# A recorder that counts TensorE's instructions in blocks of 256, and HGRN2 levels as single steps, in a hybrid decoder step

## The chip, the cores and the metric

The kernel runs on one core of one Trainium2 chip. The metric is the device time of one launch in microseconds (us). The kernel before takes 838.85 us, the median of 3 runs (838.39 to 838.94).

## What is computed

One inference step of a decoder layer for 544 token columns: a prompt of 512 tokens and 8 samples of 4 new tokens each, all in float32. The reference, cut to what matters here:

```python
h = rmsnorm(x, norm_mix); z = h @ w_in
aq, ak, av, hq, hf, hi, hg = jnp.split(z, IN_SPLITS, axis=-1)
att = dilated_attention(aq, k_all, v_all, q_idx)              # 8 heads, prompt and cached window
f = lb + (1.0 - lb) * jax.nn.sigmoid(hf)
o, s_new = hgrn2_recurrence(silu(hq) * HG_DK ** -0.5, 1.0 - f, hi, jnp.log(f), hg_s0)   # 4 heads
o = head_rmsnorm(o, hg_out_norm) * silu(hg)
x = x + concatenate([att, o]) @ w_out
x = x + cross_attention(rmsnorm(x, norm_cross), mem_k, mem_v) @ w_co
u = rmsnorm(x, norm_ffn)
x = x + (silu(causal_conv3(u @ w_gate)) * (u @ w_up)) @ w_down
y = rmsnorm(x, norm_final)
```

## The kernel before, in words

Activations lie with their features on the 128 partitions and the 544 tokens along the free axis. A dense product takes one 128-wide column strip of a weight at a time. Weight and activation are each split into a high and a low part (type fp32r), and three products, high by high, high by low and low by high, are summed in a PSUM bank. The tokens are cut into two parts of 256 and 288 (CUTS), so a *half* of a projection (w_in has 8 contraction tiles) is 24 matmuls. These dense products are the **main** steps of TensorE, and their order is fixed by the program. Everything else on TensorE is a **side** product in plain fp32: attention scores and values (psS, psT, psO), the decode attention over the cached window, whose tiles are streamed in (psd, psdo), cross-attention (ps_cp, ps_cpt, ps_cpo, ps_cs), and the HGRN2 heads.

An HGRN2 head (`hgrn`, one for each h of 0 to 3) works in levels w = 1, 2, 4 ... 64. `level_ops` makes a tile kq on VectorE and GpSimd, and `level_products` multiplies small blocks of it with each other on TensorE: 16 products of 32 columns for the levels up to 16 (one more for the samples at 1 and 2), 8 at level 32, 4 at level 64. They land in the banks psB (the diagonal, levels 1 and 2), psA (4, 8, 16) and psL (32, 64). Then come transposes and state products (pst, psin, psU, psu, pso), a norm (psr_hg), and the result om goes into the contraction of w_out (ps_wo).

The program doesn't issue instructions as it is written. `Tape` records every call as part of a `Step`; consecutive calls on TensorE of one kind (main or side) join into one step until `tape.cut()`. `Tape.order` then plays through all five engines with its own cost figures, and `Tape.run` issues the instructions in the order of the best of four such rounds. In that play TensorE takes the next main step in order, and side steps in between where they are ready:

```python
can = [s for s in waiting["PE"] if s.ready <= now + 1e-9 and fits(s)]
main = [s for s in can if s.main]
side = [s for s in can if not s.main]
if side and (burst or not main or sum(s.length for s in side) >= self.BURST
             or now - first > self.PATIENCE
             or min(s.begin for s in side) < clock[0] + now - clock[1]):
```

Each engine then has one list that it works off in order, and buffers (the tag "a" has 59) are handed out in the planned order, so a change in one list can move the others. Because every instruction is issued through `take`, nearly all rows of the profile carry its line, L621 (L597 for the DMAs).

The feed-forward stage computes gate and up projections: the first tiles plainly (ps_g, ps_u), the rest in pairs with seven block products in place of eight (ps_ag, ps_au, ps_cg, ps_cu, ps_dg, ps_du). Their weight operands S1 and S3 are sums of two blocks: one load on the SP queue, and a second, adding one on GpSimd's queue (POOL). VectorE forms S2 and S4 from them, and ScalarE (ACT) and VectorE split all of them into high and low parts (S1u4h, S2u4h, S2u4l). The products with w_down (ps_d, last ps_dz) stand between these; their activations are the tiles h0, h1 ..., split as h3h, h3l. `keep` copies a partial product out of its bank (keptg) before the bank's next product, such as S1 by T, is added.

Of the kernel before, what the change touches and what calls it, by code (L numbers as in the profile page):

```python
# [235 lines left out]
class Step:  # L236


    def __init__(self, engine, number, main):
        self.engine, self.number, self.main = engine, number, main  # L240
        self.calls, self.length, self.lag, self.bytes, self.port = [], 0.0, 0.2, 0, False
        self.deps, self.users, self.tiles = set(), [], set()
        self.gate, self.lead, self.after = None, None, set()

# [5 lines left out]
class Tape:  # L250
# [6 lines left out]

    ROUNDS = 4
    BURST, PATIENCE, SLACK, LEAD, MARGIN = 1.0, 4.0, 12.0, 15.0, 4.0
    AHEAD = {"SP": 8, "ACT": 5, "DVE": 5, "POOL": 5, "PE": 8}  # L260

    def __init__(self, nc):
# [27 lines left out]
        dims = tuple(tuple(d) for d in ap.ap)  # L290
        return name, p0, p0 + dims[0][1], _bits(dims[1:]) << f0

    def put(self, engine, call, outs, ins, length, lag=None, size=0, port=False):
        main = self.in_main and engine == "PE"
        cur = self.cur
        if not (cur is not None and cur.engine == engine and cur.main == main and (engine == "PE" or self.joined)):
            cur = self.cur = Step(engine, len(self.steps), main)
# [15 lines left out]
        cur.length += length  # L313
        cur.bytes += size
        cur.port |= port
        if lag is not None:
            cur.lag = lag
        for ap, write in [(a, False) for a in ins] + [(a, True) for a in outs]:
# [109 lines left out]
    def order(self):  # L428
# [22 lines left out]


        port = [0.0, 0.0]

        def needs(s):
            want = {}
# [24 lines left out]
            return True  # L481

        def start(s):
            nonlocal todo, bus
            waiting[s.engine].remove(s)
            for k, v in needs(s).items():
                room[k] -= v
            for n in s.tiles:
                if n in last and n not in held:
                    ends[n] = last[n]  # L490
            held.update(n for n in s.tiles if n in self.kinds)
            s.start = now
            if s.bytes:
                free[s.engine] = now + 0.4
                bus = max(bus, now) + s.bytes / 300e3
                s.end = bus + 2.0
            else:
                held_up = max(0.0, port[s.engine == "DVE"] - now) if s.port else 0.0
                if s.port:
                    port[s.engine == "POOL"] = now + held_up + s.length  # L500
                free[s.engine] = s.end = now + held_up + s.length
            if s.main:
                clock[:] = s.est, now
            for n in s.tiles:
                if n in self.kinds:
                    left[n] -= 1
                    if not left[n]:
                        ends.pop(n, None)
                        frees.append((s.end + s.lag, self.kinds[n]))
            todo -= 1  # L510
            done.append(s)
            seen = set()
            for u in s.users:
                if u in seen:
                    continue
                seen.add(u)
                if s not in u.deps:
                    at = s.start
                elif u.engine == s.engine and not s.bytes:
                    at = s.start + s.length - 0.05  # L520
                else:
                    at = s.end + s.lag
                u.ready = max(u.ready, at)
                u.waits -= 1
                if not u.waits:
                    waiting[u.engine].append(u)

        while todo:
# [12 lines left out]
            if free["PE"] <= now + 1e-9:  # L541
                can = [s for s in waiting["PE"] if s.ready <= now + 1e-9 and fits(s)]
                main = [s for s in can if s.main]
                side = [s for s in can if not s.main]
                if side and first is None:
                    first = now
                if side and (burst or not main or sum(s.length for s in side) >= self.BURST
# [15 lines left out]
                    moved = True  # L563
            if not moved:
                later = [f[0] for f in frees] + [free[e] for e in free if free[e] > now + 1e-9]
                later += [s.ready for e in waiting for s in waiting[e] if s.ready > now + 1e-9]
                if not later and self.idle < 40:

                    self.idle, clock[0] = self.idle + 1, clock[0] + 1.0
                    continue  # L570
                self.idle = 0
                assert later, "no step can begin"
                now = min(t for t in later if t > now + 1e-9)
# [3 lines left out]
class _Engine:  # L577
# [5 lines left out]
    def __getattr__(self, method):  # L583
# [3 lines left out]
        def take(*args, **kw):  # L587
# [3 lines left out]
            outs = [a for a in [kw.get("out", args[0] if args else None), kw.get("accum_out")] if hasattr(a, "ap")]  # L591
            ins = [a for a in aps if not any(a is o for o in outs)]
            n = max([int(np.prod(a.shape[1:])) for a in aps] + [1])
            lag, size, port = 0.25, 0, False
            if method == "dma_start":
                size = 4 * int(np.prod(outs[0].shape))
                return tape.put(engine, lambda: call(*args, **kw), outs, ins, 0.1, 0.3, size)  # L597
            if engine == "PE":
                n, m, k = int(np.prod(args[2].shape[1:])), outs[0].shape[0], args[1].shape[0]
                if method == "transpose":  # L600
                    n, length = 128, 0.11
                elif args[1].dtype == F32R:
                    length = 0.00046 * n + 0.001
                else:
                    length = 2 * max(0.0135, 0.00086 * n * (m / 128 if m < 128 else 1.0) * (0.5 if k <= 64 else 1.0))
                lag = 0.35
# [10 lines left out]
            else:  # L617
                port = True
                length = {"tensor_tensor": 0.2 + 0.0026 * n, "memset": 0.15 + 0.0007 * n,
                          "tensor_scalar": 0.2 + 0.0036 * n}.get(method, 0.45 + 0.0009 * n)  # L620
            return tape.put(engine, lambda: call(*args, **kw), outs, ins, length, lag, size, port)  # L621
        return take


# [1 line left out]
def tile_decoder_step(ctx: ExitStack, tc: tile.TileContext, xT, memT, kwT, vw, s0, conv_in, mkT, mv, vecs, cst,  # L626
# [619 lines left out]
    def hgrn(h, f, q, gt, v):  # L1246
# [42 lines left out]
            return kq  # L1289

        def level_products(w, kq):
            if w <= 2:
                diag_blocks(kq, kq, bank["b"], w)
                diag_sample(kq, kq, w)
# [223 lines left out]
    x = []  # L1518
# [733 lines left out]
```

## Time and profile before

| | |
|---|---|
| median of 3 runs | 838.85 us (838.39 to 838.94) |
| the profiled execution's own time | 839.05 us |
| its span in the profile | 837.3 us |
| TensorE matmuls (PE), weight loads (PEld) | 820.8 us (98%), 768.2 us (92%) |
| VectorE (DVE), ScalarE (ACT), GpSimd (POOL) | 584.8 us (70%), 398.9 us (48%), 139.0 us (17%) |

The profile is one execution, taken by the hardware profiler. Busy time is the union of an engine's instructions; matmuls are pipelined, so their rows overlap. A wait is idle time of an engine before an instruction, with what ended it: another engine's instruction, a DMA, or "issue", when the profile shows nothing that was waited for. SPq is the queue of SyncE, which issues most DMAs. Times in timelines are us from the start of the span.

### The profile page before, as it was taken

The page shows a single profiled execution, that of the slowest core. Times are in us where ns is not written, and L with a number is a line of the kernel's source. Part 1 is how long each engine was busy: PE and PEld are TensorE (multiplying, and loading weights), DVE is VectorE, ACT ScalarE, POOL GpSimd, SP SyncE. Part 2 cuts the span into 40 slices and gives each one's busy share as a digit, 9 for nine tenths or more (in the row PEclk, how much of TensorE's full clock was granted, in tenths as well). Part 3 has the DMA queues.
Part 4 walks back from the last instruction along what each step waited for, and adds up shares of the span by engine and source line. Part 5 has one row for each costly group of instructions (what it writes and reads, how often), then busy time and mean ns, then how long its engine had stood idle before and what let it go on. Part 6 is the DMA issues. An engine that isn't in the chain of part 4 may idle for free.

```text
span 837.3 us, 18858 instructions
## 1 busy us (share of the span) xinstructions
PE 820.8 (98%) x7599; PEld 768.2 (92%) x7599; DVE 584.8 (70%) x1246; ACT 398.9 (48%) x793; POOL 139.0 (17%) x239
## 2 busy tenths in 40 slices
PE   9999999999989999999999999999999999999996
PEld 9988888878788978999889998999999999999995
DVE  6775634956869996564475998977677667767754
ACT  7422323533627635453444557554455545545533
POOL 1120000110110110232133122012011210210013
PEclk9999999999999999999999999999999999999998
DMA  9647777874942544343640247556546644654503
GB/s 334 208 137 205 229 251 246 277 238 149 301 150 69 183 128 123 111 148 115 196 153 27 76 102 216 127 137 182 135 114 163 169 122 116 175 150 90 162 1 107
DMA packets 90760, 132.32 MB, mean 158 GB/s; under 512 B 6065, under 2 KB 60081, under 8 KB 90545
## 3 DMA queue, kind: packets, MB, share of 16 engines
q1 hardware_dynamic: 84480, 120.69, 45.1%
q0 software_dynamic: 5184, 9.44, 7.0%
q8 instruction: 59, 0.97, 0.4%
q10 hardware_dynamic: 1008, 0.99, 0.4%
q14 instruction: 29, 0.23, 0.1%
HBM read 123.03 MB, written 8.07 MB: 157 GB/s over the span
## 4 chain that ended last, share of the span: by engine, by line
PE 94%; DMA 3%; ACT 1%; issue 1%; DVE 0%; ACTq 0%; DVEq 0%
PE ps_d L621 13%; PE ps_au L621 6%; PE ps_ag L621 6%; PE ps_wo L621 6%; PE ps_cu L621 3%; PE ps_cg L621 3%; PE ps_k L621 3%; PE ps_q L621 3%; PE ps_hv L621 3%; PE ps_co L621 3%; PE ps_cq L621 3%; PE ps_g L621 3%; PE ps_dz L621 3%; PE ps_v L621 3%; PE ps_u L621 3%; PE ps_hf L621 2%
## 5 line engine op out<-in xcount | busy, mean ns | idle before, releaser
L621 ACT CAST wh<-wr 128x1024 fp32r<-128x1024 f32 (+1 forms) x68 | 60.9, 908 | 127.6 <-issue 15.9
L621 DVE TENSOR_TENSOR wl<-wr,wh 128x1024 fp32r<-128x1024 f32 (+1 forms) x68 | 73.1, 1085 | 13.8 <-ACT wh L621 13.3
L621 DVE TENSOR_TENSOR xr<-xr,ps_d 128x256 f32<-128x256 f32 x80 | 34.4, 433 | 36.7 <-PE ps_d L621 36.4
L621 POOL TENSOR_TENSOR hG<-hG,hf 128x256 f32<-128x256 f32 (+1 forms) x28 | 24.5, 877 | 204.9 <-DVE hf L621 132.7
L621 DVE SCALAR_TENSOR_TENSOR cv<-ug,vec,cv 128x560 f32<-128x560 f32 x44 | 35.1, 797 | 8.1 <-ACT cv L621 7.8
L621 POOL COPY last<-ug 128x2 f32<-128x2 f32 (+1 forms) x44 | 13.6, 340 | 160.7 <-DVE ug L621 133.5
L621 ACT ACTIVATE cv<-cv 128x560 f32<-128x560 f32 x22 | 14.8, 673 | 19.5 <-DVE cv L621 19.4
L621 ACT ACTIVATE cv<-ug,vec 128x560 f32<-128x560 f32 x22 | 18.8, 856 | 10.3 <-DVE ug L621 9.5
L597 POOL DMA_DIRECT2D S1u<-in_w_up x9 | 7.8, 862 | 87.6 <-DMA S1u<-in_w_up 31.0
L621 POOL TENSOR_TENSOR acc_cx<-acc_cx,sq_cx 128x256 f32<-128x256 f32 (+1 forms) x14 | 11.6, 834 | 61.8 <-ACT sq_cx L621 61.7
L621 ACT ACTIVATE P<-P,mx 128x128 f32<-128x128 f32 (+3 forms) x32 | 17.6, 552 | 5.9 <-DVE mx L621 5.9
L621 PE MATMUL ps_co<-coh,wh 128*128 128x256 f32 (+1 forms) x64 | 19.0, 298 | 0.0
L621 PE MATMUL ps_co<-col,wh 128*128 128x256 f32 (+1 forms) x64 | 18.4, 288 | 0.0
L621 PE MATMUL ps_co<-coh,wl 128*128 128x256 f32 (+1 forms) x64 | 18.4, 288 | 0.0
L621 POOL COPY ug<-conv_state 128x16 f32<-128x16 f32 x22 | 16.5, 751 | 6.1 <-PE ps_u L621 4.2
L621 DVE TENSOR_TENSOR xr<-xr,ps_wo 128x256 f32<-128x256 f32 (+1 forms) x16 | 6.8, 435 | 14.7 <-PE ps_wo L621 14.7
L621 PE MATMUL psd<-st,qbd_win 128*32 128x224 f32 x256 | 16.4, 360 | 0.0
L621 PE MATMUL psdo<-st,dpt 128*32 128x256 f32 x224 | 15.4, 385 | 0.7 <-DMA st<-in_vw 0.7
L621 DVE TENSOR_TENSOR xr<-xr,ps_dz 128x288 f32<-128x288 f32 (+1 forms) x16 | 7.0, 436 | 12.4 <-PE ps_dz L621 12.4
L621 POOL TENSOR_TENSOR acc_ux<-acc_ux,sq_ux 128x256 f32<-128x256 f32 (+1 forms) x14 | 11.9, 848 | 20.8 <-ACT sq_ux L621 20.8
L621 ACT ACT_TABLE_LOAD x11 | 14.1, 1283 | 2.3 <-issue 2.1
L621 DVE CUSTOM_DVE_ANT_0 P<-psS,bias 128x128 f32<-128x128 f32 (+3 forms) x32 | 14.2, 484 | 1.4 <-PE psS L621 1.3
(2650 smaller groups left out, 3561.5 us busy)
## 6 DMA issues: line engine op xcount, KB each, us to landing
st<-in_kwT SPq DMA_DIRECT2D x32, 448.0 KB, 5.0
st<-in_vw SPq DMA_DIRECT2D x28, 512.0 KB, 5.8
wr<-in_w_in SPq DMA_DIRECT2D x25, 512.0 KB, 5.7
wd<-in_w_down SPq DMA_DIRECT2D x32, 256.0 KB, 2.9
wrg<-in_w_gate SPq DMA_DIRECT2D x9, 512.0 KB, 5.5
wru<-in_w_up SPq DMA_DIRECT2D x9, 512.0 KB, 4.8
st<-in_mkT SPq DMA_DIRECT2D x8, 512.0 KB, 5.8
wr<-in_w_out SPq DMA_DIRECT2D x8, 512.0 KB, 3.7
```

The costliest lines, as they stand in the source:

```text
L597: return tape.put(engine, lambda: call(*args, **kw), outs, ins, 0.1, 0.3, size)
L621: return tape.put(engine, lambda: call(*args, **kw), outs, ins, length, lag, size, port)
```

## The change

Each step on TensorE now carries its number of instruction words: 4 for an fp32 product, 2 for an fp32r product or a transpose. `order` adds them up, times 1.0086, and treats the sum as cut into blocks: the first ends after 195 words, each further one after 256. When a step carries the sum over a block's end, the time of that is kept (`block_at`). `fetch` gives the earliest time at which a side step may begin: if it would cross into the next block, or come within 48 words behind such a crossing, not before the last crossing plus 6.6 us. Side steps that are earlier are left out of the choice; main steps are not held. In `level_products` a `tape.cut()` makes each level a step of its own.

```diff
--- before.py
+++ after.py
@@ -238,7 +238,7 @@
 
     def __init__(self, engine, number, main):
         self.engine, self.number, self.main = engine, number, main
-        self.calls, self.length, self.lag, self.bytes, self.port = [], 0.0, 0.2, 0, False
+        self.calls, self.length, self.lag, self.bytes, self.port, self.words = [], 0.0, 0.2, 0, False, 0
         self.deps, self.users, self.tiles = set(), [], set()
         self.gate, self.lead, self.after = None, None, set()
 
@@ -257,6 +257,9 @@
 
     ROUNDS = 4
     BURST, PATIENCE, SLACK, LEAD, MARGIN = 1.0, 4.0, 12.0, 15.0, 4.0
+
+
+    BLOCK, FIRST, WAITS, FETCH = 256, 195, 1.0086, 6.6
     AHEAD = {"SP": 8, "ACT": 5, "DVE": 5, "POOL": 5, "PE": 8}
 
     def __init__(self, nc):
@@ -290,7 +293,7 @@
         dims = tuple(tuple(d) for d in ap.ap)
         return name, p0, p0 + dims[0][1], _bits(dims[1:]) << f0
 
-    def put(self, engine, call, outs, ins, length, lag=None, size=0, port=False):
+    def put(self, engine, call, outs, ins, length, lag=None, size=0, port=False, words=0):
         main = self.in_main and engine == "PE"
         cur = self.cur
         if not (cur is not None and cur.engine == engine and cur.main == main and (engine == "PE" or self.joined)):
@@ -313,6 +316,7 @@
         cur.length += length
         cur.bytes += size
         cur.port |= port
+        cur.words += words
         if lag is not None:
             cur.lag = lag
         for ap, write in [(a, False) for a in ins] + [(a, True) for a in outs]:
@@ -451,6 +455,16 @@
 
 
         port = [0.0, 0.0]
+        words, block_at = 0.0, -100.0
+
+        def fetch(s):
+
+            n, x = s.words * self.WAITS, (self.FIRST - words) % self.BLOCK
+            if not n or x >= n + 48:
+                return 0.0, None
+            if x < n:
+                return block_at + self.FETCH - s.length * x / n, x / n
+            return block_at + self.FETCH - s.length - (x - n) / 16, None
 
         def needs(s):
             want = {}
@@ -481,7 +495,7 @@
             return True
 
         def start(s):
-            nonlocal todo, bus
+            nonlocal todo, bus, words, block_at
             waiting[s.engine].remove(s)
             for k, v in needs(s).items():
                 room[k] -= v
@@ -490,6 +504,10 @@
                     ends[n] = last[n]
             held.update(n for n in s.tiles if n in self.kinds)
             s.start = now
+            if s.words:
+                at = fetch(s)[1]
+                block_at = block_at if at is None else now + s.length * at
+                words += s.words * self.WAITS
             if s.bytes:
                 free[s.engine] = now + 0.4
                 bus = max(bus, now) + s.bytes / 300e3
@@ -541,7 +559,7 @@
             if free["PE"] <= now + 1e-9:
                 can = [s for s in waiting["PE"] if s.ready <= now + 1e-9 and fits(s)]
                 main = [s for s in can if s.main]
-                side = [s for s in can if not s.main]
+                side = [s for s in can if not s.main and fetch(s)[0] <= now + 1e-9]
                 if side and first is None:
                     first = now
                 if side and (burst or not main or sum(s.length for s in side) >= self.BURST
@@ -563,7 +581,7 @@
                     moved = True
             if not moved:
                 later = [f[0] for f in frees] + [free[e] for e in free if free[e] > now + 1e-9]
-                later += [s.ready for e in waiting for s in waiting[e] if s.ready > now + 1e-9]
+                later += [t for e in waiting for s in waiting[e] for t in (s.ready, fetch(s)[0]) if t > now + 1e-9]
                 if not later and self.idle < 40:
 
                     self.idle, clock[0] = self.idle + 1, clock[0] + 1.0
@@ -591,16 +609,17 @@
             outs = [a for a in [kw.get("out", args[0] if args else None), kw.get("accum_out")] if hasattr(a, "ap")]
             ins = [a for a in aps if not any(a is o for o in outs)]
             n = max([int(np.prod(a.shape[1:])) for a in aps] + [1])
-            lag, size, port = 0.25, 0, False
+            lag, size, port, words = 0.25, 0, False, 0
             if method == "dma_start":
                 size = 4 * int(np.prod(outs[0].shape))
                 return tape.put(engine, lambda: call(*args, **kw), outs, ins, 0.1, 0.3, size)
             if engine == "PE":
                 n, m, k = int(np.prod(args[2].shape[1:])), outs[0].shape[0], args[1].shape[0]
+                words = 4
                 if method == "transpose":
-                    n, length = 128, 0.11
+                    n, length, words = 128, 0.11, 2
                 elif args[1].dtype == F32R:
-                    length = 0.00046 * n + 0.001
+                    length, words = 0.00046 * n + 0.001, 2
                 else:
                     length = 2 * max(0.0135, 0.00086 * n * (m / 128 if m < 128 else 1.0) * (0.5 if k <= 64 else 1.0))
                 lag = 0.35
@@ -618,7 +637,7 @@
                 port = True
                 length = {"tensor_tensor": 0.2 + 0.0026 * n, "memset": 0.15 + 0.0007 * n,
                           "tensor_scalar": 0.2 + 0.0036 * n}.get(method, 0.45 + 0.0009 * n)
-            return tape.put(engine, lambda: call(*args, **kw), outs, ins, length, lag, size, port)
+            return tape.put(engine, lambda: call(*args, **kw), outs, ins, length, lag, size, port, words)
         return take
 
 
@@ -1289,6 +1308,7 @@
             return kq
 
         def level_products(w, kq):
+            tape.cut()
             if w <= 2:
                 diag_blocks(kq, kq, bank["b"], w)
                 diag_sample(kq, kq, w)
```

The change moves instructions on every engine. Three places follow. A row is line, operation, tile written and tiles read, shape, and how often; the changed program's `take` has the line L640 (L615 for DMAs).

TensorE, HGRN2 head 0 (psB, psA), the decode stream (psd) and the projections ps_q. Before:

```order
L621 MATMUL ps_q_256_218<-xm7h,wl_216 128x288
L621 MATMUL psB_174<-hq_111,hk_171 32x32 x17
L621 MATMUL psB_174<-kq_1_172 32x32 x17
L621 MATMUL psB_174<-kq_2_173 32x32 x17
L621 MATMUL psA_177<-kq_4_175 32x32 x16
L621 MATMUL psA_177<-kq_8_176 32x32 x16
L621 MATMUL ps_q_0_223<-xm0h,wh_221 128x256
```

and with the change, the 24 products of the half ps_q_256 and the 24 of ps_q_0 left out where the dots are:

```order
L640 MATMUL psB_174<-hq_111,hk_171 32x32 x17
L640 MATMUL pst_hv_190<-cs,hv_163 128x128 x4
L640 MATMUL psB_174<-kq_1_172 32x32 x17
L640 MATMUL psd_238<-st_122,qbd_win 32x224 x4
L640 MATMUL psd_238<-st_123,qbd_win 32x224 x4
L640 MATMUL psB_174<-kq_2_173 32x32 x17
L640 MATMUL ps_q_256_218<-xm0h,wh_215 128x288
...
L640 MATMUL ps_q_0_223<-xm7h,wl_222 128x256
L640 MATMUL psA_177<-kq_4_175 32x32 x16
L640 MATMUL psA_177<-kq_8_176 32x32 x16
```

Five levels in a row became three and two, with two halves of a projection between them; the three of psB begin a half earlier and have a transpose and stream products in between.

TensorE, HGRN2 head 1 (psA_381), with the stream (psdo) and projections of v and of the next head (ps_v, ps_hf). Before:

```order
L621 MATMUL ps_v_256_419<-xm7h,wl_416 128x288
L621 MATMUL psdo_429<-st_495,dpt_427 32x256 x4
L621 MATMUL psA_381<-kq_4_379 32x32 x16
L621 MATMUL psA_381<-kq_8_380 32x32 x16
L621 MATMUL psdo_429<-st_501,dpt_427 32x256 x4
L621 MATMUL pst_v_430<-cs,v_413 128x128 x4
```

and with the change, 45 products of ps_hf left out where the dots are:

```order
L640 MATMUL ps_v_256_419<-xm7h,wl_416 128x288
L640 MATMUL psB_378<-hq_343,hk_375 32x32 x17
L640 MATMUL psB_378<-kq_1_376 32x32 x17
L640 MATMUL psB_378<-kq_2_377 32x32 x17
L640 MATMUL psA_381<-kq_4_379 32x32 x16
L640 MATMUL psdo_429<-st_492,dpt_427 32x256 x4
L640 MATMUL pst_v_430<-cs,v_413 128x128 x4
L640 MATMUL psS_436<-cs,v_413 32x128
L640 MATMUL ps_hf_0_481<-xm0h,wh_479 128x256
...
L640 MATMUL ps_hf_256_484<-xm7h,wl_480 128x288
L640 MATMUL psA_381<-kq_8_380 32x32 x16
L640 MATMUL psA_381<-kq_16_385 32x32 x16
```

Levels 4 and 8 stand apart now, with both halves of ps_hf between them; psB, which stood ahead of the half ps_v_256, stands behind it.

ACT, at the start of the paired part of the feed-forward stage. Before:

```order
L621 CAST wd_0h<-wd_0_1236 128x512
L621 COPY keptg_1205<-ps_ag_1177 128x272
L621 CAST S4g4h<-S4g_1228 128x512
L621 CAST A22g4h<-A22g_1251 128x512
L621 ACTIVATE cv_1162<-cv_1162 128x560
L621 CAST wd_1h<-wd_1_1261 128x512
L621 COPY keptg_1205<-ps_ag_1177 128x272
L621 CAST S1u4h<-S1u_1241 128x512
L621 CAST h3h<-up_1166 128x544
```

and with the change:

```order
L640 CAST S1u4h<-S1u_1241 128x512
L640 COPY keptg_1205<-ps_ag_1177 128x272
L640 CAST S4g4h<-S4g_1228 128x512
L640 CAST whg_1270<-wrg_1269 128x1024
L640 ACTIVATE cv_1162<-cv_1162 128x560
L640 CAST wd_0h<-wd_0_1236 128x512
L640 COPY keptg_1205<-ps_ag_1177 128x272
L640 CAST A22g4h<-A22g_1251 128x512
L640 CAST h3h<-up_1166 128x544
```

S1u4h moved ahead of both copies keptg. On the SP queue, the load that it needs, with the semaphores (named by engine or DMA queue) that each waits for; before:

```order
L597 DMA wru_1223<-in_w_up 128x1024 [waits DMAHW4_49,DMAHW1_49,DVE_49]
L597 DMA S1u_1241<-in_w_up 128x512 [waits PE_49]
L597 DMA wd_0_1236<-in_w_down 128x512 [waits PE_49]
L597 DMA S3u_1247<-in_w_up 128x512 [waits PE_49]
L597 DMA A22g_1251<-in_w_gate 128x512 [waits DMAHW5_49,DVE_49,Pool_49]
```

and with the change:

```order
L615 DMA wru_1223<-in_w_up 128x1024 [waits DMAHW4_49,DVE_49]
L615 DMA S1u_1241<-in_w_up 128x512 [waits DMAHW2_49,DVE_49]
L615 DMA wrg_1269<-in_w_gate 128x1024 [waits DMAHW5_49,Activation_49]
L615 DMA wd_0_1236<-in_w_down 128x512 [waits PE_49]
L615 DMA S3u_1247<-in_w_up 128x512 [waits PE_49]
```

S1u's load no longer waits for TensorE but for VectorE, and the load of wrg moved up behind it.

## Rows read from the trace of the kernel before

**Rows 1.** The page, busy us (share of the span) and instructions of each engine.

```profile
PE 820.8 (98%) x7599; PEld 768.2 (92%) x7599; DVE 584.8 (70%) x1246; ACT 398.9 (48%) x793; POOL 139.0 (17%) x239
```

**Rows 2.** Waits of PE: waiting line, what ended it, us in total, times, longest.

```profile
PE psA L621 <- issue: 5.2, 3, 2.2
...
PE ps_au L621 <- ACT S2u4h L621: 0.8, 1, 0.8
PE psdo L621 <- DMA st<-in_vw: 0.7, 1, 0.7
PE ps_hf L621 <- issue: 0.5, 1, 0.5
PE ps_d L621 <- DVE h3l L621: 0.4, 1, 0.4
PE ps_d L621 <- ACT h3h L621: 0.3, 1, 0.3
PE ps_au L621 <- DVE S2u4l L621: 0.2, 1, 0.2
```

**Rows 3.** Timeline of PE at four gaps: start, us, instruction, [idle before, releaser].

```profile
49.14 0.44 PE L621 MATMUL psA<-kq 128*32 128x32 f32 x26 [1.92 <-issue]
...
171.36 0.29 PE L621 MATMUL psA<-kq 128*32 128x32 f32 x11 [1.07 <-issue]
...
177.04 0.38 PE L621 MATMUL ps_hf<-xm0h,wh 128*128 128x256 f32 x1 [0.49 <-issue]
...
235.83 0.38 PE L621 MATMUL psA<-kq 128*32 128x32 f32 x10 [2.21 <-issue]
```

**Rows 4.** The page, DMA queue of the instructions: packets, MB, share of 16 engines.

```profile
q8 instruction: 59, 0.97, 0.4%
```

**Rows 5.** Stretches between gaps: us, PE, PEld, DVE, ACT, POOL busy (instructions), PEclk, DMA.

```profile
47.30:170.20 122.90, 120.37 (x1399) 102.25 (x1399) 74.28 (x206) 42.05 (x84) 11.20 (x20) 1.00 0.71 226
170.20:176.70 6.50, 5.28 (x137) 4.43 (x127) 4.73 (x9) 1.66 (x7) 2.60 (x4) 1.00 1.05 330
176.70:233.70 57.00, 56.58 (x636) 45.82 (x636) 37.58 (x101) 26.21 (x52) 3.73 (x5) 1.00 0.68 220
```

**Rows 6.** The same view, of the stretches just ahead of three gaps.

```profile
46.00:47.30 1.30, 1.22 (x131) 1.10 (x117) 0.79 (x2) 0.76 (x1) 0.41 (x2) 1.00 0.81 275
165.10:170.20 5.10, 5.10 (x124) 4.33 (x111) 3.65 (x12) 1.00 (x1) 1.90 (x3) 1.00 1.09 351
231.40:233.70 2.30, 2.22 (x129) 1.53 (x115) 2.14 (x5) 1.60 (x4) 0.00 (x0) 1.00 1.13 358
```

**Rows 7.** The chain that ended last, 75 to 86 us: start, us, what.

```profile
75.66 3.39 PE ps_k L621 x24
...
79.56 3.04 PE ps_k L621 x24
```

**Rows 8.** Timeline of PE at 45.5 us, from main to side products.

```profile
45.50 0.29 PE L621 MATMUL ps_q<-xm7h,wl 128*128 128x288 f32 x1
45.72 0.27 PE L621 MATMUL psB<-hq,hk 128*32 128x32 f32 x8
```

**Rows 9.** Waits of SPq, timelines of SP, ACT and PE, and the chain, 495 to 514 us.

```profile
SPq L597 <- PE ps_u L621: 14.9, 2, 14.5
...
501.94 0.33 SPq L597 DMA_DIRECT2D S1u<-in_w_up  x1
...
505.14 8.41 DMA S1u<-in_w_up
...
495.17 0.65 ACT L621 CAST h2h<-up 128x544 fp32r<-128x544 f32 x1 [0.41 <-DVE up L621]
...
507.95 0.38 ACT L621 COPY keptg<-ps_ag 128x272 f32<-128x272 f32 x1
...
513.62 0.62 ACT L621 CAST S1u4h<-S1u 128x512 fp32r<-128x512 f32 x1 [2.64 <-DMA S1u<-in_w_up]
...
508.78 0.28 PE L621 MATMUL ps_ag<-Th,S1g4h 128*128 128x272 f32 x1
```

## The prediction

> **What bounds the kernel now.** First the page's busy times: TensorE's matmuls cover 820.8 of 837.3 us, no other engine more than 70% [rows 1]. The kernel ends when TensorE has worked off its list, so only two things can shorten it: less TensorE work, or less TensorE idling. Second, who TensorE waits for [rows 2]. The rows shown that name another engine or a DMA sum to 2.4 us; two others, 5.2 and 0.5 us, name "issue": nothing that the profile shows was missing. Third, TensorE's timeline at those gaps [rows 3]: 1.92, 1.07, 0.49 and 2.21 us, together 5.7 us, and each stands in or just behind the level products of an HGRN2 head (psA, psL), all in the first 236 us.
>
> Where they stand is the key. The instruction queue moved 59 packets, 0.97 MB, so 16.4 KB each [rows 4]. TensorE has 7,599 matmuls and as many weight loads [rows 1], 15,198 words; over 59 packets that is 257.6 a packet. Between the first gap and the second lie 1,399 weight loads, to the third 127, to the fourth 636 [rows 5]. Doubled for the matmuls: 2,798, 254 and 1,272, which is 10.9, 1.0 and 5.0 times 256, each 1% short, as it must be if some words (waits) are in no row. So a gap stands only where a block of 256 words ends, and it is the wait for the next block.
>
> How long is a fetch? A block that begins asks for the next; where TensorE had to wait, the distance from the block's start to the gap's end is the fetch. The windows that hold about 128 matmuls (131, 124, 129) ahead of a gap start at 46.0, 165.1 and 231.4 us [rows 6], and the gaps end at 49.14, 171.36 and 235.83 [rows 3]: 3.1, 6.3 and 4.4 us. The third block starts as the second gap ends and its own ends at 177.04: 5.7 us. One half of a projection (24 matmuls, 48 words) takes 3.0 to 3.4 us [rows 7], so a block of main products alone lasts 16 us and hides any of these. A block of level products (51 in psB are 204 words) lasts 1.2 us, from 46.0 to the start of the gap at 47.22.
>
> **The change, part by part.** It adds and drops no arithmetic: both orders have 5,618 rows of products on TensorE. It moves them, and the hold is a matter of the plan: no instruction waits for anything new when it runs. Five prices, against the profiled execution (839.05 us, 0.2 above the median of the runs; the sum is then taken off the median).
>
> 1. *The four gaps go.* In the new order head 0 has two halves (6.4 us) between its psB and psA products, where none stood; the levels of heads 1, 2 and 3 are broken at two places each by one or two halves. Taken away: 5.7 us.
>
> 2. *What is left of them.* Counted in words from the first boundary (195, then every 256), the shortest blocks of the new order are the one that starts in head 1's psB, and those near head 3's psB and head 2's psB. The first holds some 26 psB, 16 psA and three small sides, then 28 main products. For the sides I take 2.2 us, near the 2.3 us of the old block that also held levels and two small sides (the last of [rows 6]); the main products are 28 times 0.13, 3.6. So 5.8 us against a fetch of 6.3 at the longest: 0.5 us of gap. The others hold more main products and come out at 6.2 us and above. I take +0.4; the bounds are 0 (fetches of 3 to 5 us) and +1.5 (all three 0.5 short).
>
> Here the Trainium skill speaks against the change: its page "Runtime: NRT & Kernel Launch", section "Instruction fetch mechanics", has blocks of 256 instructions too, but gives TensorE room for 2,048 of them and calls the crossing of a block mostly hidden. By that rule terms 1 and 2 would be nothing and the sum -0.2 us. For 55 of 59 packets the trace agrees with "hidden"; for the four gaps it does not.
>
> 3. *Switching.* A half's last product is followed 0.22 us later by the first side product [rows 8], where main products follow each other at 0.13 to 0.14 [rows 7]: 0.1 us, and I take as much for the way back. The new order has one round trip more (53 against 52). +0.2 us, bounds 0 and +0.6 for the extra changes from one kind of side to another.
>
> 4. *New short waits.* Every engine's list was planned anew. In the cross-attention several value products (ps_cpo) now stand one or two short products behind the transposes whose copy they read, and head 3's psr_hg only six products behind pso. A copy of 128x512 on ACT takes 0.62 us [rows 9], so each of some four places can cost 0.1 to 0.3. The only wait of that sort before the feed-forward stage is now the 0.7 us for a stream tile [rows 2], and its place moves too. +0.5 us, bounds -0.7 (that wait goes) and +1.5. Head 3's chain gets no later for w_out: after its last side product 30 instead of 24 ps_cv products remain.
>
> 5. *Start of the feed-forward stage.* Now SP sends the first S1u load at 501.94, after 14.5 us of waiting for the last ps_u product; POOL's adding transfer onto it goes out at 505.14 and takes 8.41 us among the loads that SP sends in one burst; ACT, which works in order, sits 2.64 us before S1u4h, with h3h and S2u4h behind it [rows 9]. TensorE then waits 0.8, 0.2, 0.4 and 0.3 us for these, 1.7 in all [rows 2]. In the new order h2h, cast at 495.17 before, comes later (behind S1g4h), so S1u can have a buffer of that time, and its load waits for DVE and no more for TensorE, so it should land some microseconds earlier, outside the burst. The S2u4 waits (1.0) should go, the h3 ones may stay, since ACT has more ahead of h3h. I take -0.9; bounds -1.7 and 0.
>
> Sum: -5.7 + 0.4 + 0.2 + 0.5 - 0.9 = **-5.5 us, 833.4 us**. All lower bounds together give -8.1, all upper ones -2.1. What hides the moved products is slack in the HGRN2 chains: they feed w_out at 328 us, and only head 3 is near it.
>
> **Rivals.**
>
> *The fetch is slower than the new spacing.* The gaps fell where the DMA queues were full, and the new order puts other transfers beside the same heads. For it: 6.3 us was seen, the new blocks are near that. Against it: it must exceed the spacing by a whole microsecond several times. If half of the 5.7 us stays: -5.5 + 2.85, about 836.2 us. Chance 0.12, mostly still faster.
>
> *The gaps are not the fetch.* TensorE would stop in the levels for another reason, say the hand-over of 32-column products, and holding them back would only move the stop. Then terms 3 to 5 alone remain: -0.2, 838.7 us. For it: all four gaps are in psA or psL. Against: three distances that are multiples of 256 within 1%, and head 3's levels, which do not gap. Chance 0.06. The Trainium skill's page named above would lead to this time.
>
> *ACT is blocked.* ACT's list now has S1u4h ahead of the copy keptg, which frees the bank for the S1 by T product (ps_ag, 508.78 us). If S1u lands as late as now (513.54), that copy comes at 514.24 (513.62 + 0.62) and not at 507.95, 6.3 us later; 0.45 of it is slack (it ends at 508.33 now), so TensorE stands 5.8 us [rows 9], from which the 1.7 of term 5 come off: -5.7 + 0.4 + 0.2 + 0.5 + 5.8 - 1.7 = -0.5, 838.4 us. Each microsecond that it lands later costs one more: from 2.2 us later (515.7) the change is slower by over 0.2%, and at 3 us later, which a load stuck behind a late DVE release and then the burst would give, it is 841.4 us. Against it: SP waited 14.5 us before that load, so one that does not need the last ps_u product has room. Chance 0.09, of which 0.05 slower.
>
> **How the numbers follow.** The forecast has 0.73. 0.2% (1.7 us) is about what a measurement of this kernel can tell from no change. Faster by over that: the forecast and three quarters of the first rival (0.09), 0.82. Within it: the rest of that rival, the second, and the third at its smaller price, 0.13. Slower: 0.05. The range for 8 in 10 runs from 831.0 (all of term 5 and the stream wait gone) to 837.0 (all upper bounds, or half of the gaps left).
>
> **What would show it.** Right: TensorE's waits for "issue" fall from 5.7 to under 1 us; still 59 instruction packets; psA and psL rows with halves of ps_q, ps_hf or ps_ck between them and no gap; S1u's load issued before the last ps_u product; S2u4 out of TensorE's waits. Step 2 is wrong if gaps of over 0.5 us remain at block ends; step 4, if ps_cpo or psr_hg appear with over 1.5 us; step 5, if ACT still waits for S1u. The forecast as a whole is wrong if the gaps go and the time does not: then the 5.7 us have turned into waits elsewhere, and TensorE's list of waits names where.

## The result, and the profile after

The changed kernel takes 831.39 us, the median of 6 runs (830.23 to 832.56). The kernel before, run beside it, takes 838.83 us (838.39 to 841.37, 6 runs). The ratio is 0.9905, 95% interval 0.9888 to 0.9922. On the first median that is 830.9 us: faster, as forecast, by 8.0 us and not 5.5, just under the range's low end of 831.0. The two medians differ by 7.4 us, and the two profiled executions by 7.1, in their own times (839.05 and 831.95) and in their spans (837.3 and 830.2). The account below is of these 7.1 us; the 0.9 up to the 8.0 lies within the spread of the runs, and no trace accounts for it.

From the page of the changed kernel: busy times, the instruction queue, and the chain that ended last, by engine.

```profile
PE 820.8 (99%) x7599; PEld 767.0 (92%) x7599; DVE 584.1 (70%) x1246; ACT 400.1 (48%) x793; POOL 143.4 (17%) x239
...
q8 instruction: 59, 0.97, 0.5%
...
PE 97%; DMA 1%; DVE 1%; ACT 0%; issue 0%; DVEq 0%; POOLq 0%; ACTq 0%
```

TensorE is busy for as long as before, 820.8 us [rows 1], and the instruction queue moves the same 59 packets [rows 4]. So the whole gain is idle time. It fell from 16.5 to 9.4 us (span less busy). These are all of TensorE's waits in the changed kernel: line, what ended it, us in total, times, longest.

```profile
PE ps_first L640 <- DVE zero L640: 1.1, 1, 1.1
PE ps_ag L640 <- ACT keptg L640: 1.1, 1, 1.1
PE psr_final L640 <- ACT sq_last L640: 0.2, 1, 0.2
```

The first and the last also stood before. Against [rows 2] the list gives an account with no rest to speak of: "issue" 5.7 to 0 us, the wait for the stream tile 0.7 to 0, the start of the feed-forward stage 1.7 to 1.1. Together that is 7.0 of 7.1 us.

The 1.1 us is the third rival in small. The chain of the changed kernel at that place, start, us, what:

```profile
492.41 3.59 DMA S1u<-in_w_up
...
496.53 6.75 DMA S1u<-in_w_up
...
503.30 0.02 ACT S1u4h L640
...
503.83 0.39 ACT keptg L640
```

S1u's load left SP 9.5 us earlier than before (501.94, [rows 9]), but ACT reached S1u4h before GpSimd's adding transfer had landed, and keptg stood behind it.

**What the account doesn't show: the clock.** The granted clock of the kernel before, in stretches behind the fourth gap (us, PE busy, granted clock as a share of full speed, DMA share, GB/s):

```profile
236.00:238.00 2.00, 2.00 (x21) 0.50 0.79 279
238.00:239.00 1.00, 1.00 (x7) 0.58 0.06 25
239.00:241.00 2.00, 2.00 (x18) 1.00 0.00 0
```

For more than 2.5 us TensorE ran at the lower of its two levels, 1.2 GHz. What that cost stands in the chain of the same kernel, which has the same 48 products at either level:

```profile
177.04 6.31 PE ps_hf L621 x48
236.59 7.25 PE ps_hf L621 x48
```

0.94 us, within busy time and in no list of waits. In the changed kernel the clock stays up there:

```profile
225.00:240.00 15.00, 15.00 (x282) 1.00 0.58 183
```

So about 1 us of busy time went, and as the total stands still, about as much came in elsewhere; where is not shown.

### The profile page after: what moved, and what is told of

It reads as the page before. It is cut to its first block, busy times and chain, and to the rows that moved or that the text cites. A ratio compares the mean times of both kernels' runs of the same rounds, so it can differ in the third digit from the quotient of the medians.

```text
span 830.2 us, 18833 instructions
## 1 busy us (share of the span) xinstructions
PE 820.8 (99%) x7599; PEld 767.0 (92%) x7599; DVE 584.1 (70%) x1246; ACT 400.1 (48%) x793; POOL 143.4 (17%) x239
## 4 chain that ended last, share of the span: by engine, by line
PE 97%; DMA 1%; DVE 1%; ACT 0%; issue 0%; DVEq 0%; POOLq 0%; ACTq 0%
PE ps_d L640 13%; PE ps_au L640 7%; PE ps_ag L640 6%; PE ps_wo L640 6%; PE ps_cu L640 3%; PE ps_cg L640 3%; PE ps_hv L640 3%; PE ps_k L640 3%; PE ps_q L640 3%; PE ps_co L640 3%; PE ps_v L640 3%; PE ps_cq L640 3%; PE ps_g L640 3%; PE ps_first L640 3%; PE ps_dz L640 3%; PE ps_hf L640 2%
## 5 line engine op out<-in xcount | busy, mean ns | idle before, releaser
L640 ACT CAST wh<-wr 128x1024 fp32r<-128x1024 f32 (+1 forms) x68 | 60.6, 907 | 118.8 <-PE ps_q L640 21.9
L640 DVE TENSOR_TENSOR wl<-wr,wh 128x1024 fp32r<-128x1024 f32 (+1 forms) x68 | 72.2, 1071 | 11.0 <-ACT wh L640 10.3
L640 POOL TENSOR_TENSOR hG<-hG,hf 128x256 f32<-128x256 f32 (+1 forms) x28 | 26.2, 937 | 190.1 <-DVE hf L640 129.2
L640 DVE TENSOR_TENSOR xr<-xr,ps_d 128x256 f32<-128x256 f32 x80 | 34.4, 433 | 25.5 <-PE ps_d L640 25.2
L640 POOL COPY last<-ug 128x2 f32<-128x2 f32 (+1 forms) x44 | 16.8, 411 | 159.5 <-DVE ug L640 141.3
L640 DVE SCALAR_TENSOR_TENSOR cv<-ug,vec,cv 128x560 f32<-128x560 f32 x44 | 35.1, 798 | 6.5 <-ACT cv L640 6.0
L640 ACT ACTIVATE cv<-cv 128x560 f32<-128x560 f32 x22 | 14.8, 673 | 29.0 <-DVE cv L640 29.0
L640 ACT ACTIVATE cv<-ug,vec 128x560 f32<-128x560 f32 x22 | 18.8, 856 | 10.3 <-DVE ug L640 9.4
L640 POOL TENSOR_TENSOR acc_cx<-acc_cx,sq_cx 128x256 f32<-128x256 f32 (+1 forms) x14 | 11.7, 836 | 60.2 <-ACT sq_cx L640 60.1
L615 POOL DMA_DIRECT2D S1u<-in_w_up x9 | 7.8, 862 | 79.8 <-DVE wlu L640 31.2
L640 PE MATMUL ps_co<-coh,wh 128*128 128x256 f32 (+1 forms) x64 | 19.1, 298 | 0.0
L640 ACT ACTIVATE P<-P,mx 128x128 f32<-128x128 f32 (+3 forms) x32 | 17.6, 550 | 2.7 <-DVE mx L640 2.7
L640 PE MATMUL ps_co<-col,wh 128*128 128x256 f32 (+1 forms) x64 | 18.4, 288 | 0.0
L640 PE MATMUL ps_co<-coh,wl 128*128 128x256 f32 (+1 forms) x64 | 18.4, 288 | 0.0
L640 DVE TENSOR_TENSOR xr<-xr,ps_wo 128x256 f32<-128x256 f32 (+1 forms) x16 | 6.8, 435 | 15.6 <-PE ps_wo L640 15.6
L640 PE MATMUL psd<-st,qbd_win 128*32 128x224 f32 x256 | 16.2, 359 | 0.0
L640 POOL COPY ug<-conv_state 128x16 f32<-128x16 f32 x22 | 13.8, 626 | 13.7 <-PE ps_au L640 8.9
L640 PE MATMUL psdo<-st,dpt 128*32 128x256 f32 x224 | 15.8, 386 | 0.0
L640 DVE TENSOR_TENSOR xr<-xr,ps_dz 128x288 f32<-128x288 f32 (+1 forms) x16 | 7.0, 437 | 12.3 <-PE ps_dz L640 12.2
L640 DVE CUSTOM_DVE_ANT_0 P<-psS,bias 128x128 f32<-128x128 f32 (+3 forms) x32 | 14.2, 485 | 0.6 <-PE psS L640 0.4
L640 POOL TENSOR_TENSOR acc_ux<-acc_ux,sq_ux 128x256 f32<-128x256 f32 (+1 forms) x14 | 11.2, 799 | 19.2 <-ACT sq_ux L640 19.2
```

## The experiments

Three theories stood against each other. **A**: the gaps are waits for the next block of 256 instruction words. **B**: they belong to the level products as they were recorded, and single steps end them wherever blocks begin. **C**: a gap of about 2 us also drops the granted clock. **D** came later: the rest of the gain is an accident of the plan. Every run stood beside runs of the kernel before, whose median was 839.61 us in runs 1 to 4, 839.64 in 5 to 8 and 838.79 in 9 to 11.

**1. The changed kernel, block starts moved.**

```diff
-BLOCK, FIRST, WAITS, FETCH = 256, 195, 1.0086, 6.6
+BLOCK, FIRST, WAITS, FETCH = 256, 324, 1.0086, 6.6
+            for _ in range(32):
+                nc.tensor.matmul(banks[0][1][:, :8], zero[:, :128], zero[:, :8], start=True, stop=True)
             warm_up(WARM)
```

> The changed kernel, every engine's order the same, with 128 more instruction words of TensorE (32 tiny products of zeros) ahead of its first warm-up, where it waits for the first data anyway; the recorder's FIRST is moved by the same count, so that it still plans as if the blocks of 256 began where they did. Theory A (the four gaps of the kernel before were waits for the next block of 256 words): the holding back now protects the wrong places, so gaps come back where two real block starts lie close together: worked out from the order and the durations of the kernel before, with a fetch of 4.5 to 6.5 us, at head 0's psB products (1.2 to 3.2 us) and head 1's psA products (1.0 to 3.0 us), perhaps 1 us at head 2; in sum 2 to 8 us of PE waits with releaser issue, time 833.5 to 838, and none at the three places where the kernel before had them in heads 0 and 2 at psA. Theory B (the gaps came from the way the level products were recorded, whole levels in one call, and went because they are now single steps): no gap, 831.4 within 0.5. Theory C (clock: the gap of 2.2 us ahead of psA of head 2 dropped the granted clock to 0.5 for 3.4 us): any returning gap of about 2 us or more is followed by a stretch with a granted clock near 0.5, a gap of 1 us or less is not.

Measured: 844.97 us, ratio 1.0068 (1.0048 to 1.0088). No "issue" gap at all, so A missed here. The time says nothing of the gaps: the 32 products weren't free. They stand in the groups of this run, ahead of the first data, with 13.8 us:

```profile
L641 PE MATMUL ps_first<-zero 128*128 128x8 f32 x64 | 13.8, 361 | 1.1 <-DVE zero L641 1.1
```

**2. The kernel before, block starts moved** by the same 32 products.

> The kernel before with the same 32 tiny products ahead of the first warm-up, nothing else: blocks of 256 words begin 128 words earlier in the program. Theory A (waits for blocks): the gap ahead of head 0's psA (1.9 us) is gone or below 0.3, the one ahead of head 2's psA (2.2 us) is gone or below 1.7, the gaps of head 1 move (ps_v1_256 or psA1, 0.6 to 2.7 each), and head 3, which had none, gets one of 3.3 to 5.3 us at its psA or psL products near 295 us. Time 835 to 840. Theory B (gaps belong to the level products of heads 0, 1 and 2 as recorded): the same four gaps at the same products, 838.8 within 0.6. Theory C (the clock): no fall of the granted clock at 235 to 239 us, but one right after the large gap of head 3, which costs about 1 us beside the gap itself.

Measured: 849.64 us, ratio 1.0133 (1.0106 to 1.0160). The gaps moved, as A says: TensorE's waits in this run have them at ps_v (head 1) and at psA, this time of head 3; heads 0 and 2 have none. The profiled execution is the longest of the six (855.85 us), so its DMA waits need not be those of the median; the 32 products stand in the time as in run 1.

```profile
PE ps_v L622 <- issue: 2.1, 1, 2.1
PE psA L622 <- issue: 2.0, 1, 2.0
PE psd L622 <- DMA st<-in_kwT: 1.8, 1, 1.8
```

Behind each of these three waits, one of them for a DMA, the granted clock fell, in stretches of the same run:

```profile
133.00:136.00 3.00, 3.00 (x30) 0.50 0.97 275
188.00:190.00 2.00, 2.00 (x27) 0.50 0.55 163
314.00:317.00 3.00, 3.00 (x25) 0.50 0.09 27
```

**3. Single steps alone:** the kernel before with `tape.cut()` at the head of `level_products`.

> The kernel before with the one line in the level products alone (each level's products as single steps), no counting and no holding back. Theory A: the level products are spread among main products by this already, so most gaps go, but nothing protects the block starts: left over 0.5 to 4 us in heads 1 and 3 (ps_v1_256 and psO3 by the order); time 831 to 835. Theory B (single steps alone do it): no gap, 831.4 within 0.5. If the counting does all the work: gaps of 5 us and more, 836 to 839.

Measured: 833.84 us, ratio 0.9936 (0.9916 to 0.9956). One gap of 0.3 us is left. But the other waits of the kernel before are there too, except the 0.3 us for h3h, and the one for the stream tile is longer:

```profile
PE psdo L621 <- DMA st<-in_vw: 1.5, 3, 0.8
...
PE ps_au L621 <- ACT S2u4h L621: 0.8, 1, 0.8
PE ps_d L621 <- DVE h3l L621: 0.4, 1, 0.4
PE ps_v L621 <- issue: 0.3, 1, 0.3
PE ps_au L621 <- DVE S2u4l L621: 0.2, 1, 0.2
```

**4. Holding back alone:** the changed kernel without that `tape.cut()`.

> The changed kernel without the one line that makes the level products single steps: the counting and holding back alone. Theory A: whole levels can be held back too, and nothing but the block starts matters: no gap, or one below 1 us in head 0 or 3; time 830.5 to 832.5. If the levels as one step are too long to be placed between two block starts, one gap of 1 to 2 us stays in a head and the time is 832.5 to 835. Fewer changes between kinds of products than with single steps: if these changes cost the time that the forecast lacks, PE's busy time in the HGRN part (150 to 320 us) is 0.5 to 1 us below that of the changed kernel.

Measured: 833.78 us, ratio 0.9934 (0.9918 to 0.9950), above what was expected. No gap. Again the feed-forward start (1.6 us), the stream tile (0.7) and a new short wait (psT for a copy, 0.6) are there. So either half of the change takes the gaps away in the order that it leads to, and neither median gives the other 2 us (the intervals of runs 3 and 4 touch that of the changed kernel, 0.9888 to 0.9922, so the waits tell more here than the times). PE's busy time is 820.3 us, 0.5 below the changed kernel's.

**5 and 6. Block starts moved without the 13 us.** The first warm-up (40 words) is replaced by 30 (run 5, changed kernel, FIRST 276) or 42 (run 6, kernel before) small products:

```diff
-            warm_up(WARM)
+            for _ in range(30):
+                nc.tensor.matmul(banks[0][1][:8, :8], zero[:, :8], zero[:, :8], start=True, stop=True)
```

> The changed kernel, every engine's order the same, but its first warm-up of 10 products (40 words) is replaced by 30 products of 8 columns by 8 (120 words), so every block of 256 words of TensorE begins 80 words earlier in the program than the recorder plans for (FIRST is moved by the same count, which keeps the plan). Two block starts then lie about 1.2 us of products apart at head 1's psdo and psA products near 166 us, which is closer than in the first shifted run (3.6 us apart there, no wait). Theory A (a start waits until the block, asked for when the block ahead was entered, is there, 3.1 to 6.3 us later): one gap of PE with releaser issue of 2.0 to 3.5 us there, and none or one under 0.7 elsewhere. Theory B (single steps alone make the gaps go, wherever blocks begin): no gap. Theory C (the granted clock falls to 0.5 for some 3 us after a gap of about 2 us): it falls after this gap, and PE's busy time is 1.0 to 1.5 us above the changed kernel's 820.8, less or more what the other first warm-up takes. Time with gap and fall 834 to 836.5, without either 831.5.

Measured: 833.40 us, ratio 0.9923 (0.9905 to 0.9941), no gap: A missed again, with two starts 1.2 us apart. TensorE waited 2.2 us more for the first data, since these warm-ups are over sooner.

> The kernel before, every engine's order the same, its first warm-up of 40 words replaced by 42 products of 8 by 8 (168 words): block starts 128 words earlier, as in the second run, without the 13 us that its 32 wide products cost ahead of the first product. Theory A: no gap at head 0's psA (47 us) and none at head 2's psA (233 us); one of about 2 us at ps_v of head 1 near 170 us and one of about 2 us at psA of head 3 near 296 us. Theory B: the four gaps of the kernel before. Theory C: the granted clock falls after each gap of about 2 us, PE's busy time goes up by 1.0 to 1.5 us for each fall more than the one of the kernel before. Time 836 to 839.

Measured: 839.18 us, ratio 0.9991 (0.9976 to 1.0006). TensorE's order is that of the kernel before, product by product (a few rows of ScalarE and VectorE did move, other than the expectation says), and the gaps moved. The timeline of PE in run 6 (heads 1, 1 and 3):

```profile
168.95 0.30 PE L622 MATMUL ps_v<-xm6l,wh 128*128 128x288 f32 x1 [1.70 <-issue]
...
173.57 0.22 PE L622 MATMUL psL<-kq 128*32 128x32 f32 x2 [0.79 <-issue]
...
295.28 0.23 PE L622 MATMUL psA<-kq 128*32 128x32 f32 x3 [1.93 <-issue]
```

Heads 0 and 2 have none, and the time is just above the 836 to 839 expected. B can't make a gap of head 3 out of unchanged level products; A can. The clock fell after the last of the three (296 to 300 us at 0.57) and not after the one of 1.70.

**7 and 8. FETCH at 6.4 and at 9.0**, nothing else.

> The changed kernel with FETCH at 6.4 in place of 6.6. The plan keeps the block starts as far apart, but comes out with the order of the kernel before at the start of the feed-forward part on ScalarE (keptg, then S1u4h) and another order of side products in the HGRN part. Theory D (the 0.7 us at the feed-forward start and the 0.7 us of psdo's wait for its stream tile are by-products of where the plan happens to fall): no issue gap of PE, waits for h3h, h3l, S2u4h and S2u4l of 1.6 to 1.8 us in sum as in the kernel before, a wait for st of 0 to 1.5 us, time 831.8 to 833.5. Rival (the holding back itself gives them): waits there as in the changed kernel, 1.1 us, time 831.4 within 0.5.

> The changed kernel with FETCH at 9.0: side products are held back for longer after each block start. If 6.6 left block starts that cost a little without showing as a wait, this gains up to 0.5; by the gaps seen (none at 6.6) it has nothing to win: no issue gap, or one below 0.5; PE's busy time within 0.7 of 820.8; the order at the feed-forward start is that of the kernel before again (1.6 to 1.8 us of waits). Time 831.5 to 833.5.

Measured: 832.79 us, ratio 0.9918 (0.9902 to 0.9933), and 834.33 us, 0.9933 (0.9916 to 0.9950). Neither has an "issue" gap. In run 7 most of the waits that the changed kernel had lost are back:

```profile
PE ps_au L640 <- ACT S2u4h L640: 0.8, 1, 0.8
PE psdo L640 <- DMA st<-in_vw: 0.7, 2, 0.5
...
PE ps_d L640 <- DVE h3l L640: 0.4, 1, 0.4
```

That is D, by the waits; by the times run 7 (0.9902 to 0.9933) can't be told from the changed kernel. Holding back longer (run 8) came out above the 833.5 us expected, with a wait of its own, 1.2 us of TensorE for VectorE's hk.

**9 to 11. The same shift of 56 words for three kernels**, by 14 of the small products ahead of the first warm-up: single steps alone; the changed kernel with a wrong FIRST (251), so in its old order; and the changed kernel, which counts the 14 and plans anew.

> The kernel with single steps alone (third run), with 14 products of 8 by 8 (56 words, under 1 us) ahead of the first warm-up: block starts 56 words earlier, nearly the same order. By the order and the durations two starts then lie 2.1 us of products apart at head 1's psA (near 164 us, where the DMA engines were busy all the time in the third run), others 2.1 us at head 2's hf product near 236 us and 2.4 us at head 3's psA near 295 us. Theory A, with the size learnt from the runs before (a fetch starts 0 to 5 us after the block ahead is entered, later where the DMA engines are full, and the start goes on 2.2 to 2.7 us after the fetch begins): one gap of 1 to 4 us of releaser issue at 164 us, perhaps a second below 2 us near 236; none where the DMA engines are idle. Single steps alone then only happened to lie well. Theory B (single steps are enough wherever blocks begin): no gap over 0.5 us. Time by A 835 to 838, by B 834.

> The changed kernel with the same 14 products of 8 by 8 ahead, FIRST moved so that the recorder plans as if the blocks began where they did: same order, block starts 56 words earlier than planned for, two of them 2.1 us of products apart at head 1's pst_v, psdo and psA near 167 us, the next closest 2.4 us near 288 us. Theory A: a gap of 0.5 to 4 us near 167 us if the DMA engines are full there (0.8 and more in the stretch before), none if they are not, as in the fifth run, where starts lay 1.2 us apart at a DMA share of 0.26 to 0.73 and nothing waited. Theory B: no gap. Time 831.5 to 836.

> The changed kernel with the same 14 products ahead, and FIRST as it is, so that the recorder counts them and plans for where the blocks do begin. Theory A: no gap over 0.5 us anywhere, whatever the DMA engines do, since no two starts lie closer than 4.8 us; the feed-forward start is ordered as in the kernel before (1.6 to 1.8 us of waits), time 832 to 834. If it shows gaps as the tenth run does, the holding back is not what keeps them away.

Measured: 837.99 us, ratio 0.9984 (0.9972 to 0.9995); 831.32 us, 0.9914 (0.9895 to 0.9932); 833.28 us, 0.9937 (0.9918 to 0.9955). Run 9 has one gap, the largest of all (the profiled execution, 836.07 us, is the shortest of the ten). Its timeline of PE, then its clock and DMA share ahead of and behind the gap:

```profile
167.70 0.28 PE L622 MATMUL psA<-kq 128*32 128x32 f32 x9 [3.14 <-issue]
```

```profile
162.00:164.40 2.40, 1.88 (x105) 1.00 1.04 370
167.70:169.00 1.30, 1.30 (x17) 1.00 1.11 350
169.00:172.00 3.00, 3.00 (x14) 0.50 0.64 205
```

Single steps were enough in run 3 only because block starts happened to lie well; moved by 56 words, nearly the whole gain is lost. (TensorE's order in run 9 differs from run 3's only between 58 and 83 us, far ahead of the gap.) Run 10 has starts about as close (1.9 us) and no gap, at a lower DMA share:

```profile
162.50:165.40 2.90, 2.90 (x51) 1.00 0.19 77
165.40:169.00 3.60, 3.60 (x152) 1.00 0.42 130
```

Run 5 is alike where its starts are closest:

```profile
165.00:168.00 3.00, 3.00 (x152) 1.00 0.09 30
```

The instruction queue's own packets show what varies. In run 9, the 0.1 us from 165.0 to 165.1 (packets, MB, share):

```profile
q8 instruction: 1, 0.02, 67.8%
```

There is none in the 1.0 us before, so the fetch begins here, and TensorE goes on at 167.70, 2.6 to 2.7 us later. In the kernel before the packet of the fourth gap begins at 233.3 to 233.4 us, and TensorE goes on at 235.83, 2.4 to 2.5 later. That part is nearly constant: each of the ten gaps of 0.4 us and more in the kernel before and runs 2, 6 and 9 ends 2.2 to 2.7 us after such a packet begins. What varies is how long the packet takes to begin. In run 9, with the DMA engines full, it came when the short block was already over. In run 5 it came about 1.4 us ahead of the short block, from 165.1 to 165.2 us:

```profile
q8 instruction: 1, 0.02, 80.0%
```

Full DMA engines are not the whole reason, though. The last gap of run 6 has its packet from 293.0 to 293.1 us, about 1.1 us into a block as short as that of run 5, with the DMA engines nearly idle; run 2's gap in head 3 (310.93 to 312.96 us) is the same. The stretches of both, run 6 first (the last number but one is the DMA share):

```profile
291.00:293.20 2.20, 2.20 (x168) 1.00 0.07 14
```

```profile
309.00:310.00 1.00, 1.00 (x81) 1.00 0.00 0
310.00:311.00 1.00, 0.93 (x100) 1.00 0.09 16
```

Each cost about 2 us all the same. Ahead of these two blocks TensorE worked on side products (psdn, psO), ahead of those of runs 5 and 10 on main ones (ps_v). But main products (ps_q) stood ahead of the first gap of the kernel before too, at a DMA share of 0.81 [rows 6] and [rows 8]. Which of the two brings the packet early was not tried, so why close starts cost nothing in runs 1, 5 and 10 stays open.

Run 11 has no gap, at a place where run 9 had 3.1 us and the DMA engines were as full (1.08 from 162 to 169 us, as against 1.07 to 1.10). So starts that are kept apart did without luck here, at one place of one order. Its feed-forward start and stream tile cost 1.4 and 1.0 us.

## Why the forecast had the sign right and the gain too small

- **Term 1, the four gaps, -5.7: right**, in size and cause. Run 6 moves the gaps by moving block starts with TensorE's order unchanged, runs 2 and 9 with the order around the gaps unchanged. The Trainium skill's page "Runtime: NRT & Kernel Launch", section "Instruction fetch mechanics", calls the crossing mostly hidden and gives TensorE 2,048 instructions of room; by that the time would have stayed where it was. The blocks of 256 agree with the runs, the room doesn't show: starts 1.2 us apart cost 1.9 us of waiting [rows 3].
- **Term 2, +0.4 left over: 0.** It took the longest fetch seen (6.3 us) for every close pair. That length was seen with full DMA engines only, and closeness alone doesn't set the cost: a pair 1.2 us apart cost nothing in run 5 and 1.9 us in run 6, at DMA shares of 0.09 and 0.07.
- **Term 4, new short waits, +0.5: -0.7.** This is the step that failed, 1.2 us of the miss of 1.6 between the profiles. No new wait came, and the one for the stream tile went, which the forecast had as its bound. Runs 3, 4, 7 and 11 (0.7 to 1.5 us at that tile) show that this isn't a property of the change. It isn't one of the order either: runs 1, 5 and 10, in the changed kernel's order, wait 0.8, 0.5 and 0.6 us for a stream tile. That the term came out at its bound was luck.
- **Term 5, feed-forward start, -0.9: -0.6.** The S2u4 and h3 waits went, and 1.1 us for keptg came, by the mechanism of the third rival. With the order that the plan gives at a FETCH of 6.4 little is won there (1.4 us of waits of the 1.7); in the changed kernel's own order the wait for keptg is 0.4 us in run 1, 1.3 in run 5 and none in run 10.
- **Term 3, switching, +0.2: not separated.** Busy time is unchanged in total, about -1.0 for the clock and about +1.0 for the rest. But run 10, in the same order, has 820.4 us with 14 products more, so differences of half a microsecond lie within what executions of one order show. By tile, TensorE is busy for 8.6 us with ps_cpo where it was 7.2, and for 4.9 with ps_cs where it was 4.1; rows of different tiles overlap, so that is a place to look and no sum.
- **Left out: the clock.** The half-speed stretch was in the trace of before, right behind the fourth gap, and the sum had no term for it. A gap of 2.2 us was worth about 3.

The low end of 831.0 took terms 4 and 5 whole; with terms 2 and 3 at nothing too, the forecast's own lower bounds (-8.1) reach 830.8 us, so the range was cut a little shorter than its sum. Orders without a gap over 0.3 us gave 831.3 to 834.3 us (run 1 aside, with its 13.8 us); that spread is what a new plan does, whatever it is for. No version beats the changed kernel: run 10 (831.32 us) is the same order and can't be told from it.

## What to carry to other kernels

A wait that no row explains can be the instruction stream: count the words between such gaps, see whether the distance is a multiple of a block, and whether each gap ends at a constant time behind a packet of the instruction queue. The clean test is to move the block starts and nothing else, with a few tiny products ahead of the first data, and it needs several shifts, since a close pair doesn't cost something every time: starts 1.2 us apart cost 1.9 us in run 6 and nothing in run 5. And look at the granted clock behind every gap before pricing it: half speed afterwards is busy time and stands in no list of waits.

## What the runs showed of the hardware that was not expected

The granted clock fell to half after waits of 1.8, 1.9, 2.0, 2.1, 2.2 and 3.1 us, and not after others of 1.7 and 1.9: length alone doesn't decide it. In run 11 it fell with no wait at all. Its stretches, the first of them filled with products of 16 to 128 columns (psin, pso, psds):

```profile
309.00:313.00 4.00, 4.00 (x35) 1.00 0.43 125
...
314.00:317.00 3.00, 3.00 (x8) 0.50 0.00 0
```

TensorE was busy throughout. Why it fell there was not tried. And ahead of the first data a product of 8 columns was no cheaper than one of 128 while its weights had 128 columns: the 64 halves of run 1 (an fp32 product is two rows) took 13.8 us, 0.22 each, and the 20 of the first warm-up, of 128 columns, 0.23 each, where the 60 of run 5 with 8-column weights took 1.7 us by its groups. The first warm-up in the timeline of the kernel before, and the group of run 5:

```profile
1.06 4.64 PE L621 MATMUL ps_first<-zero 128*128 128x128 f32 x20 [1.06 <-DVE zero L621]
```

```profile
L641 PE MATMUL ps_first<-zero 128*8 128x8 f32 x60 | 1.7, 171 | 1.1 <-DVE zero L641 1.1
```
